# Operand addresses of the matrix products, the order of score groups and one engine choice in a hybrid attention block

## The chip, the cores and the metric

The kernel runs on one core of a Trainium2 chip. The metric is the device time of one execution in microseconds; of the kernel before, three executions were timed (median 804.39, from 802.62 to 804.96). A profile comes from one further execution.

## The reference

One decoder block, 512 tokens, width 2048. A normalised input is projected; half of the heads (A: 8 heads of 128, two key/value heads) use compressed, selected and windowed attention, the other half (B: 16 heads of 64) use a window of 128 with sinks. Each half is gated by a SiLU path, and both go through one output projection.

```python
h = _rmsnorm(x, norm_g[l])
proj = h @ w_in[l]
...
kc = _compress(_rope(_heads(kca, N_KV_A, HEAD_DIM_A)), cmp_k_pos[l], cmp_k_w1[l], cmp_k_w2[l])
vc = _compress(_heads(vca, N_KV_A, HEAD_DIM_A), cmp_v_pos[l], cmp_v_w1[l], cmp_v_w2[l])
o_cmp, p_cmp = _compressed_attention(qa, kc, vc)
sel_idx = _select_blocks(p_cmp, S)
o_sel = _selected_attention(qa, _rope(_heads(ksa, N_KV_A, HEAD_DIM_A)), _heads(vsa, N_KV_A, HEAD_DIM_A), sel_idx)
o_win = _banded_attention(qa, _rope(_heads(kwa, N_KV_A, HEAD_DIM_A)), _heads(vwa, N_KV_A, HEAD_DIM_A), WIN_A)
gates = jax.nn.sigmoid(ga.astype(jnp.float32)).reshape(B, S, N_KV_A, GROUP_A, 3).astype(x.dtype)
o_a = gates[..., 0:1] * o_cmp + gates[..., 1:2] * o_sel + gates[..., 2:3] * o_win
y_a = o_a.reshape(B, S, WIDTH_A) * jax.nn.silu(za)
...
o_b = _banded_attention(qb, _rope(_heads(kb, N_KV_B, HEAD_DIM_B)), _heads(vb, N_KV_B, HEAD_DIM_B),
                        WIN_B, sink=sinks[l].reshape(N_KV_B, GROUP_B))
y_b = o_b.reshape(B, S, WIDTH_B) * jax.nn.silu(zb)
x = x + jnp.concatenate([y_a, y_b], axis=-1) @ w_out[l]
return _rmsnorm(x, final_g)
```

With 512 tokens there are 8 blocks of 64 and 16 may be selected, so every block is, and the selected attention is causal attention over all tokens.

## The kernel before

All of it is one function, `hybrid_block`. A float32 operand is split into two float32r "words", a high word (made on ScalarE, L97 and L542) and the low word that remains (a subtraction on VectorE, L99 and L543). `mm3` (L118 to L121) makes a product of two split operands as three matrix products: high by high, high by low, low by high. Each has a still operand, 128 columns that are loaded into the array, and a moving operand of 256, 280, 288 or 512 columns.

The stages, with their place in the profile:

- 0 to 291 us: projections with the normalised input as the moving operand, 512 columns wide (`proj`, L119 to L121 into `pj`), and the 8 pairs of B heads among them: scores (L349, L350), transposes of the probabilities (L384), values (L389, L390).
- 291 to 316 us, first V stage: `tok_chunk` multiplies tokens (still) by weights (moving, words from `words(MOVING)`), 256 columns wide; among them `compress_unit` (L708, L709) for the compressed keys, words from `words(BELOW)`.
- 316 to 352 us, second V stage: the same with 280 columns (values and gates), among them the compression of the values.
- 352 to 425 us: `seven`, a product of 2x2 blocks in seven block products instead of eight, for the A keys; its words come from `words(STILL)` and stand still, combinations of the input (`xh`, `xl`, `pu`, `qw`) move, 256 columns wide.
- 425 to 665 us: for each A head, `pair` (queries and gate by `seven`; `turn` and `q_split` rotate and split the query, on POOL for heads 0 to 5) and `attn_a`: scores (L932) against the key words `KH`, `KL` in runs of three passes, for each of four query tiles; transposes (L969, L981, L983); values (L975 to L977, L990, L992). A tile scheduler interleaves one head's attention with the next head's `seven`.
- 665 to 801 us: the output projection, y words still, weight words moving, then the final norm.

A run of scores has one, two or three column groups: 288 columns (32 compressed keys and 256 keys), then 256 or 512, then in the last query tile another 256. `step` (L125 to L127) adds one product whose result is not used, with chosen operand addresses, at the start of the first V stage, in `keys` and in the output stage.

Where a tile stands is set by the order in which pools are opened and tiles taken from them; small tiles named `space` move those behind them. `words(place)` cuts 1,024 columns out of tiles of 1,088 at an offset of `place` columns of 4 bytes:

```python
MOVING, EVEN, STILL, BELOW = 0, 16, 32, 48
...
def words(place):
    return [wp.tile([P, 1088], F32R, name=nm, tag=nm)[:, place:place + 1024] for nm in ("whi", "wlo")]
```

Of the kernel before, what the change touches and what calls it, by code (L numbers as in the profile page):

```python
# [10 lines left out]
F32 = mybir.dt.float32  # L11
F32R = mybir.dt.float32r
# [5 lines left out]
P = 128  # L18
S = 512
D = 2048  # L20
KT = D // P
# [6 lines left out]
CMP = 32  # L28
MOVING, EVEN, STILL, BELOW = 0, 16, 32, 48
WARM = 40  # L30
# [5 lines left out]
def hybrid_block(ctx, tc, xT, xtm, w0, wv0, wv1, wz, wq, wo0, wos, cw1, cw2, cpos, e2, rope, tabs, sinks, gT, fg, out):  # L36
# [5 lines left out]

    const = ctx.enter_context(sb("const"))
    wp = ctx.enter_context(sb("wp", bufs=3))
    ident = const.tile([P, P], F32, name="ident")
# [4 lines left out]
    bmask = tab[:, 512 + NQ * CMP:768 + NQ * CMP]  # L50
    small = const.tile([P, 8], F32, name="small")
    rstd, eps = small[:, 0:NQ], small[:, NQ:NQ + 1]
    rstdb = const.tile([P, S], F32, name="rstdb")
    gates = const.tile([P, NQ, 24], F32, name="gates")
    gt = const.tile([P, KT + 1], F32, name="gt")
    rowvalid = gt[:, KT:KT + 1]

# [49 lines left out]
    xpool = ctx.enter_context(sb("xpool", side="right"))  # L107
    xh = xpool.tile([P, KT, S], F32R, name="xh")
    xl = xpool.tile([P, KT, S], F32R, name="xl")
    angles = xstack.enter_context(sb("angles", side="right"))  # L110
# [11 lines left out]

    flat = xh.rearrange("p k s -> p (k s)")

# [19 lines left out]
    def load_x(k):  # L144
        xr = tmp("xr")
        if k == 0:
            nc.sync.dma_start(gt, gT)
        nc.sync.dma_start(xr, xT[:, k, :])
        last["xh"] = act.activation(xh[:, k, :], xr, AF.Copy, scale=gt[:, k:k + 1]).ins
        return xr  # L150
# [48 lines left out]
    with tc.issue_after(last["dma"]):  # L199
        nc.sync.dma_start(cosB, rope[:, 2, :])  # L200
        nc.sync.dma_start(sinB, rope[:, 3, :])
        nc.sync.dma_start(tab, tabs)
    dve.tensor_tensor(out=cosB, in0=cosB, in1=rstdb, op=ALU.mult)
    dve.tensor_tensor(out=sinB, in0=sinB, in1=rstdb, op=ALU.mult)
# [86 lines left out]

    vbf = wb.tile([P, NQ, P], F32, name="vbf")
    sk = wb.tile([P, 5, 16], F32, name="sk")
    nc.sync.dma_start(sk[:, 0, :], sinks)
    act.activation(sk[:, 1, :], sk[:, 0, :], AF.Copy, scale=-1.0)
    KBH = wb.tile([P, 2, S], F32R, name="KBH")
    KBL = wb.tile([P, 2, S], F32R, name="KBL")
    VB = wb.tile([P, NQ, 2, P], F32R, name="VB")
# [34 lines left out]
    def softmax_b(i, q2):  # L333
# [4 lines left out]
        for part in range(2):  # L338
            sums = wk.tile([P, 3, 2, 2], F32, name="sums", tag="sums")
            mn, dn, ex = sums[:, 0], sums[:, 1], sums[:, 2]  # L340
            for e in range(2):
                qt = 2 * part + e
                tt = wb.tile([P, 2, 256], F32, name="ttb", tag="ttb", bufs=6)
                tts.append(tt)
                ko = max(qt - 1, 0) * P
                qs = slice(qt * P, (qt + 1) * P)
                sp = pssb.tile([P, 2, 256], F32, name="spb", tag="spb")
                for v in range(2):
                    pe.matmul(sp[:, v, :], q2[v][:, qs], KBH[:, g, ko:ko + 256], start=v == 0, stop=False)  # L349
                    pe.matmul(sp[:, v, :], q2[v][:, qs], KBL[:, g, ko:ko + 256], start=False, stop=v == 1)  # L350
                n = 256 if qt else 128
                for v in range(2):
                    dve.tensor_tensor_reduce(out=tt[:, v, 0:n], in0=sp[:, v, 0:n], in1=bmask[:, 256 - n:256],
                                             scale=-SCALE_B, scalar=1e38, op0=ALU.add, op1=ALU.min,
                                             accum_out=mn[:, e, v:v + 1])
            dve.tensor_tensor(out=mn, in0=mn, in1=nskb, op=ALU.min)  # L356
            dve.tensor_tensor(out=ex, in0=mn, in1=skb, op=ALU.add)
            act.activation(ex, ex, AF.Exp)
            for e in range(2):
                n = 256 if part or e else 128  # L360
                for v in range(2):
                    tv = tts[2 * part + e][:, v, 0:n]
                    act.activation(tv, tv, AF.Exp, bias=mn[:, e, v:v + 1], scale=-1.0, accum_out=dn[:, e, v:v + 1])  # L363
            dve.tensor_tensor(out=dn, in0=dn, in1=ex, op=ALU.add)
            dve.reciprocal(dn, dn)
            for e in range(2):
                n = 256 if part or e else 128
                for v in range(2):
                    tv = tts[2 * part + e][:, v, 0:n]
                    dve.tensor_scalar(tv, tv, dn[:, e, v:v + 1], None, op0=ALU.mult)  # L370
# [125 lines left out]
    VF = kv.tile([P, 2, 2, 256], F32, name="VF")  # L496
    VC = [kv.tile([P, P], F32R, name=f"VC{g}") for g in range(2)]
    ahead = ExitStack()
    quarters = [ahead.enter_context(sb(f"ahead{e}", side="right")).tile([P, 1024], F32, name=f"ahead{e}") for e in range(2)]
# [171 lines left out]
    def pair(h, hooks=None, extra=None):  # L671
        def q_done(qv):
            turn(qv, engine=pool if h < 6 else dve)
            return q_split(qv, pool if h < 6 else dve)

# [142 lines left out]
    early, ready = quarters[:1], quarters[1:]  # L818
    places = [words(MOVING), words(BELOW), words(BELOW)]

# [24 lines left out]
    for u in range(8):  # L845
# [5 lines left out]
        if u == 0:  # L851
# [3 lines left out]
            cacc[1] = bank(4)  # L855
        compress_unit(1, u, cacc[1], words(BELOW))
        if 1 <= u <= 3:
# [28 lines left out]
    kv = kvstack.enter_context(sb("kvK", side="right"))  # L886
    KH, KL = [kv.tile([P, CMP + 1056], F32R, name=f"K{e}")[:, 0:CMP + 1024] for e in "HL"]
    for e, k in enumerate((KH, KL)):
# [20 lines left out]
    def attn_a(h, qh, ql, st):  # L909
# [4 lines left out]
        for pair in range(2):  # L914
            tt = wa.tile([P, 1792 if pair else 768], F32, name=f"tt{pair}", tag=f"tt{pair}")
            sums = wk.tile([P, 2, 2, 3], F32, name="sums", tag="sums")
            mn, dn = sums[:, 0], sums[:, 1]
            views = []
            off = 0
            for i in range(2):  # L920
# [6 lines left out]
                if qt == 3:  # L927
                    groups.append((1024, 1280, 800))
                qs = slice(qt * P, (qt + 1) * P)
# [70 lines left out]

    yh, yl = [[w[:, (2 * f + 1) % 17, :] for f in range(16)] for w in (xh, xl)]

# [148 lines left out]
    for c, u, ms in ((0, 0, ()), (0, 1, ()), (0, 2, ()), (1, 0, (0, 1, 2)), (1, 1, (3, 4)), (1, 2, (5, 6)), (0, 3, ()),  # L1151
                     (1, 3, (7,))):
        hi, lo = load_unit(wo0[:, c, u], 1024, place=MOVING, loaded=first_units.pop(0) if first_units else None, after=last["qh"],
                           after_lo=low_y[11] if (c, u) == (0, 2) else last["turn"])
# [9 lines left out]
        with tc.issue_after(words_of), tc.issue_after(last["gate", 1]):  # L1164
            for m in ms:
                combos(m)
    banks1 = banks(1)
    step(banks1[3], flat[:, 3 * S - 16:3 * S + 112], flat[:, 2 * S + 32:2 * S + 288])
    for T in range(2):
# [30 lines left out]
    def halves(raw, to=None):  # L1200
        hi, lo = to or words(MOVING)
        split_to(hi, lo, raw)
        return hi, lo
# [5 lines left out]
    for n in range(1, 4):  # L1209
# [117 lines left out]
        else:  # L1327
# [8 lines left out]
            def pair():  # L1336
                return words(MOVING)

# [181 lines left out]
```

## Time and profile before

| | |
|---|---|
| median of three runs | 804.39 us |
| the profiled execution | 802.8 us |
| its span, first to last instruction | 801.0 us |
| mean granted TensorE clock | 0.997 |
| matrix products in it | 5,693 |
| DMA traffic | 131.05 MB, mean 164 GB/s |

The span is what the profile's page and the trace's views divide; 1.8 us of the profiled execution lie around it. A product's recorded duration is longer than the distance to the next one's start, since products are pipelined; the distance is read from two start times, or from a stretch's length and the number of products in it. PE is the matrix product, PEld the load of its still operand, DVE is VectorE, ACT ScalarE, POOL GpSimd, SP the queue engine.

### The profile page before, as it was taken

How to read it: one execution, taken by the hardware profiler on the slowest of the kernel's cores; microseconds unless marked ns; L12 is line 12 of the kernel's file. 1: busy time of each engine (PE TensorE's matmuls, PEld its weight loads, DVE VectorE, ACT ScalarE, POOL GpSimd, SP SyncE). 2: the span in 40 equal slices, each digit the busy share in tenths (PEclk: the TensorE clock that was granted, in tenths of full speed). 3: DMA queues.
4: the chain of work that ended last, by engine and by line, in shares of the span. 5: the costliest groups of instructions: out<-in, count | busy, mean ns of one | idle time of the engine just before them, and what ended most of it. 6: DMA issues, size and time to landing. Idle time of an engine off the chain costs nothing.

```text
span 801.0 us, 15316 instructions
## 1 busy us (share of the span) xinstructions
PE 789.6 (99%) x5693; PEld 739.1 (92%) x5693; DVE 686.3 (86%) x1407; ACT 504.7 (63%) x1103; POOL 108.3 (14%) x111
## 2 busy tenths in 40 slices
PE   9999999999999999999999999999999999999996
PEld 8788888888888899999999999999999999999996
DVE  7668988889989597759999999998999798978895
ACT  6646657655666356664447778777777867553545
POOL 3615002110121000323210110110100000000000
PEclk9999999999999999999999999999999999999998
DMA  7572243564373469887723213225216836797845
GB/s 239 172 242 81 79 144 106 171 171 150 101 210 106 158 200 281 257 269 194 207 82 106 68 53 119 82 92 159 71 50 216 296 120 219 257 266 193 258 86 211
DMA packets 49563, 131.05 MB, mean 164 GB/s; under 512 B 6000, under 2 KB 8848, under 8 KB 49488
## 3 DMA queue, kind: packets, MB, share of 16 engines
q1 hardware_dynamic: 43376, 110.89, 42.3%
q0 software_dynamic: 5824, 18.65, 10.5%
q8 instruction: 45, 0.74, 0.4%
q10 hardware_dynamic: 288, 0.52, 0.2%
q14 instruction: 30, 0.25, 0.1%
HBM read 113.23 MB, written 16.81 MB: 162 GB/s over the span
## 4 chain that ended last, share of the span: by engine, by line
PE 86%; DVE 6%; DMA 3%; ACT 2%; issue 2%; POOL 0%; SPq 0%; DVEq 0%; ACTq 0%
PE pj L119 16%; PE pj L121 15%; PE pj L120 15%; PE oa L120 5%; PE oa L119 5%; PE oa L121 5%; PE sp L932 4%; PE bank L121 2%; PE bank L120 2%; PE bank L119 2%; DMA xr<-xT 2%; DVE wlo L543 2%; PE tp L969 2%; PE tp L384 2%; DMA raw<-wq 1%
## 5 line engine op out<-in xcount | busy, mean ns | idle before, releaser
L119 PE MATMUL pj<-xh,whi 128*128 128x256 f32 (+1 forms) x592 | 196.9, 333 | 0.6 <-ACT t L608 0.5
L121 PE MATMUL pj<-xh,wlo 128*128 128x256 f32 (+1 forms) x592 | 196.2, 331 | 0.0
L120 PE MATMUL pj<-xl,whi 128*128 128x256 f32 (+1 forms) x592 | 196.1, 331 | 0.0
L119 PEld LDWEIGHTS pj<-xh,whi 128*128 128x128 f32 x592 | 111.4, 188 | 11.0 <-ACT t L608 0.9
L121 PEld LDWEIGHTS pj<-xh,wlo 128*128 128x128 f32 x592 | 111.4, 188 | 10.1
L120 PEld LDWEIGHTS pj<-xl,whi 128*128 128x128 f32 x592 | 111.4, 188 | 9.7
L543 DVE TENSOR_TENSOR wlo<-raw,whi 128x1024 fp32r<-128x1024 f32 (+2 forms) x80 | 92.9, 1172 | 7.8 <-ACT whi L542 7.2
L542 ACT ACTIVATE whi<-raw 128x1024 fp32r<-128x1024 f32 (+2 forms) x80 | 77.6, 985 | 30.7 <-DVE raw L581 11.5
L99 DVE TENSOR_TENSOR wlo<-raw,whi 128x1024 fp32r<-128x1024 f32 (+1 forms) x61 | 72.1, 1184 | 22.8 <-ACT whi L97 22.3
L97 ACT ACTIVATE whi<-raw 128x1024 fp32r<-128x1024 f32 (+1 forms) x60 | 56.6, 945 | 28.8 <-PE pj L120 14.8
L120 PE MATMUL oa<-wlo,xh 128*128 128x256 f32 x200 | 55.5, 278 | 0.0
L119 PE MATMUL oa<-whi,xh 128*128 128x256 f32 x200 | 55.4, 278 | 0.0
L121 PE MATMUL oa<-whi,xl 128*128 128x256 f32 x200 | 55.2, 276 | 0.0
L121 PE MATMUL pj<-pu,wlo 128*128 128x256 f32 x160 | 45.0, 281 | 0.5 <-DVE wlo L543 0.5
L119 PE MATMUL pj<-pu,whi 128*128 128x256 f32 x160 | 45.1, 282 | 0.4 <-DVE zr L581 0.4
L120 PE MATMUL pj<-pu,whi 128*128 128x256 f32 x160 | 44.7, 279 | 0.0
L289 DVE TENSOR_TENSOR pl<-tp,ph 128x512 fp32r<-128x512 f32 (+1 forms) x64 | 40.7, 651 | 3.1 <-ACT ph L288 2.9
L288 ACT ACTIVATE ph<-tp 128x512 fp32r<-128x512 f32 (+1 forms) x64 | 34.1, 560 | 9.6 <-PE tp L969 4.4
L363 ACT ACTIVATE ttb<-ttb,sums 128x256 f32<-128x256 f32 (+1 forms) x64 | 30.0, 471 | 14.4 <-DVE sums L356 14.4
L121 PEld LDWEIGHTS oa<-whi,xl 128*128 128x128 f32 x200 | 37.6, 188 | 0.0
L120 PEld LDWEIGHTS oa<-wlo,xh 128*128 128x128 f32 x200 | 37.6, 188 | 0.0
L119 PEld LDWEIGHTS oa<-whi,xh 128*128 128x128 f32 x200 | 37.5, 188 | 0.0
(401 smaller groups left out, 2369.8 us busy)
## 6 DMA issues: line engine op xcount, KB each, us to landing
raw<-wq SPq DMA_DIRECT2D x41, 512.0 KB, 4.4
raw<-wz SPq DMA_DIRECT2D x36, 512.0 KB, 4.0
cw<-cw SPq DMA_DIRECT2D x32, 256.0 KB, 4.0
raw<-wos SPq DMA_DIRECT2D x14, 512.0 KB, 5.9
rw<-wos SPq DMA_DIRECT2D x10, 512.0 KB, 4.8
xr<-xT SPq DMA_DIRECT2D x16, 256.0 KB, 3.4
rows<-xT SPq DMA_DIRECT2D x8, 512.0 KB, 4.7
raw<-wo SPq DMA_DIRECT2D x8, 512.0 KB, 6.0
```

The costliest lines, as they stand in the source:

```text
L97: last["hi"] = act.activation(hi[:, :width], rw[:, :width], AF.Copy).ins
L99: last["lo"] = dve.tensor_tensor(out=lo[:, :width], in0=rw[:, :width], in1=hi[:, :width].bitcast(F32), op=ALU.subtract).ins
L119: pe.matmul(ps, ah, bh, start=first, stop=False, skip_group_check=go_on)
L120: pe.matmul(ps, ah, bl, start=False, stop=False, skip_group_check=go_on)
L121: recent["mm"] = pe.matmul(ps, al, bh, start=False, stop=last, skip_group_check=go_on).ins
L288: act.activation(ph, tp, AF.Copy)
L289: dve.tensor_tensor(out=pl, in0=tp, in1=ph.bitcast(F32), op=ALU.subtract)
L363: act.activation(tv, tv, AF.Exp, bias=mn[:, e, v:v + 1], scale=-1.0, accum_out=dn[:, e, v:v + 1])
L384: pe.transpose(tp[:, o:o + P], tts[kt + s][:, v, c0:c0 + P], ident)
L542: split_hi = act.activation(hi, src, AF.Copy).ins
L543: last["lo"] = dve.tensor_tensor(out=lo, in0=src, in1=hi.bitcast(F32), op=ALU.subtract).ins
L932: pe.matmul(sp[:, a:b], qq[:, qs], kk[:, ko:ko + b - a], start=pi == 0, stop=pi == 2)
```

## The change

The change moves operands to other addresses, changes the order of the column groups in the last query tile's scores, gives head 0's rotation and split to VectorE, and loads one column of the gain tile apart. The number and the shapes of the products are the same.

The addresses modulo 256 bytes, moving operand / still operand, as the built programs have them:

| products | before | after |
|---|---|---|
| 512-wide projections | 192 / 192 | same |
| B scores (L349, L350) | 192 / 0 | same |
| B transposes (L384), B values (L389, L390) | 128 / 192 | 192 / 0 |
| V stages, tokens by weights | 128 / 192 | same |
| compression (L708, L709) | 64 / 128 | 128 / 192 |
| `seven` | 192 / 0 | same |
| A scores, the 288-column group | 192 / 0 | 0 / 0 |
| A scores, the other groups | 64 / 0 | 128 / 0 |
| A transposes, A values | 128 / 192 | 192 / 0 |
| output products | 128 / 192 | 192 / 0 |
| the unused product of the output stage | 64 / 128 | 128 / 192 |

The core of the diff:

```diff
-MOVING, EVEN, STILL, BELOW = 0, 16, 32, 48
+MOVING, EVEN, STILL = 0, 16, 32
...
     const = ctx.enter_context(sb("const"))
+    gt = const.tile([P, KT], F32, name="gt")
...
-    small = const.tile([P, 8], F32, name="small")
+    small = const.tile([P, 16], F32, name="small")
...
-    gt = const.tile([P, KT + 1], F32, name="gt")
-    rowvalid = gt[:, KT:KT + 1]
+    rowvalid = small[:, 8:9]
...
-    xh = xpool.tile([P, KT, S], F32R, name="xh")
-    xl = xpool.tile([P, KT, S], F32R, name="xl")
+    slabs = xpool.tile([P, 2 * KT * S + 64], F32R, name="x")
+    xh, xl = [slabs[:, e * KT * S:(e + 1) * KT * S].rearrange("p (k s) -> p k s", s=S) for e in range(2)]
...
-            nc.sync.dma_start(gt, gT)
+            nc.sync.dma_start(gt, gT[:, 0:KT])
...
         nc.sync.dma_start(tab, tabs)
+        nc.sync.dma_start(rowvalid, gT[:, KT:KT + 1])
...
-    vbf = wb.tile([P, NQ, P], F32, name="vbf")
+    vbf = wb.tile([P, NQ, P], F32, name="vbf", tag="ob")
+    KBH = wb.tile([P, 2, S], F32R, name="KBH")
+    KBL = wb.tile([P, 2, S], F32R, name="KBL")
     sk = wb.tile([P, 5, 16], F32, name="sk")
...
-            sums = wk.tile([P, 3, 2, 2], F32, name="sums", tag="sums")
+            sums = wk.tile([P, 6, 2, 2], F32, name="sums", tag="sums")
...
     VC = [kv.tile([P, P], F32R, name=f"VC{g}") for g in range(2)]
+    kv.tile([P, 48], F32, name="space")
...
         def q_done(qv):
-            turn(qv, engine=pool if h < 6 else dve)
-            return q_split(qv, pool if h < 6 else dve)
+            turn(qv, engine=pool if 0 < h < 6 else dve)
+            return q_split(qv, pool if 0 < h < 6 else dve)
...
-    places = [words(MOVING), words(BELOW), words(BELOW)]
+    places = [words(MOVING) for n in range(3)]
...
-        compress_unit(1, u, cacc[1], words(BELOW))
+        compress_unit(1, u, cacc[1], words(MOVING))
...
-    KH, KL = [kv.tile([P, CMP + 1056], F32R, name=f"K{e}")[:, 0:CMP + 1024] for e in "HL"]
+    KH, KL = [kv.tile([P, CMP + 1056], F32R, name=f"K{e}")[:, 16:CMP + 1040] for e in "HL"]
+    kv.tile([P, 16], F32, name="space")
...
-            sums = wk.tile([P, 2, 2, 3], F32, name="sums", tag="sums")
+            sums = wk.tile([P, 4, 2, 3], F32, name="sums", tag="sums")
...
                 if qt == 3:
-                    groups.append((1024, 1280, 800))
+                    groups.insert(1, (1024, 1280, 800))
...
-    yh, yl = [[w[:, (2 * f + 1) % 17, :] for f in range(16)] for w in (xh, xl)]
+    yh, yl = [[slabs[:, (e * KT + (2 * f + 1) % 17) * S + 16:][:, 0:S] for f in range(16)] for e in range(2)]
...
-        hi, lo = load_unit(wo0[:, c, u], 1024, place=MOVING, ...
+        hi, lo = load_unit(wo0[:, c, u], 1024, place=EVEN, ...
...
+    cmb.tile([P, 48], F32, name="space3")
     banks1 = banks(1)
-    step(banks1[3], flat[:, 3 * S - 16:3 * S + 112], flat[:, 2 * S + 32:2 * S + 288])
+    step(banks1[3], flat[:, 2 * S:2 * S + P], flat[:, 3 * S - 16:3 * S + 240])
...
-        hi, lo = to or words(MOVING)
+        hi, lo = to or words(EVEN)
...
-                return words(MOVING)
+                return words(EVEN)
```

VectorE before, behind the last rotation of head 0 (`t` is the query, `zr` the gate path, `raw` and `wlo` weights of head 1; rows are line, operation, output and inputs, shape):

```order
L581 TENSOR_TENSOR zr<-zr,pj 128x256
L543 TENSOR_TENSOR wlo<-raw,whi 128x1024
L677 TENSOR_TENSOR zr<-zr,rstdb 128x512
L581 TENSOR_TENSOR raw<-raw 128x1024
L682 SCALAR_TENSOR_TENSOR st<-st,zr 128x512
L581 TENSOR_TENSOR raw<-raw 128x1024
```

The same place of VectorE after; a line of before stands here one or two numbers higher:

```order
L583 TENSOR_TENSOR zr<-zr,pj 128x256
L545 TENSOR_TENSOR wlo<-raw,whi 128x1024
L666 TENSOR_TENSOR t_4495<-t_4495,t_4691 128x512
L679 TENSOR_TENSOR zr<-zr,rstdb 128x512
L583 TENSOR_TENSOR raw<-raw 128x1024
L262 TENSOR_TENSOR ql<-t_4495,qh 128x512
L684 SCALAR_TENSOR_TENSOR st<-st,zr 128x512
L583 TENSOR_TENSOR raw<-raw 128x1024
```

The rotation's last addition stands ahead of the gate path's product, the query's low word behind it and one addition of weights; both were POOL's. On TensorE, the scores of head 0's last query tile before, with the product of head 1's projection on each side:

```order
L121 MATMUL pj<-xh,wlo 128x256
L932 MATMUL sp<-KH,qh 128x288
L932 MATMUL sp<-KH,qh 128x512
L932 MATMUL sp<-KH,qh 128x256
L932 MATMUL sp<-KL,qh 128x288
L932 MATMUL sp<-KL,qh 128x512
L932 MATMUL sp<-KL,qh 128x256
L932 MATMUL sp<-KH,ql 128x288
L932 MATMUL sp<-KH,ql 128x512
L932 MATMUL sp<-KH,ql 128x256
L119 MATMUL pj<-xh,whi 128x256
```

and the same run after:

```order
L121 MATMUL pj<-x,wlo 128x256
L935 MATMUL sp<-KH,qh 128x288
L935 MATMUL sp<-KH,qh 128x256
L935 MATMUL sp<-KH,qh 128x512
L935 MATMUL sp<-KL,qh 128x288
L935 MATMUL sp<-KL,qh 128x256
L935 MATMUL sp<-KL,qh 128x512
L935 MATMUL sp<-KH,ql 128x288
L935 MATMUL sp<-KH,ql 128x256
L935 MATMUL sp<-KH,ql 128x512
L119 MATMUL pj<-qw_608,whi 128x256
```

Each pass now ends with 512 columns, and the run stands one `mm3` of head 1's projection later. From here on the scheduler's interleaving of attention and projection differs in places; behind the last attention the output stage's products stand in the same order.

More of the change, by code (lines that the diff above doesn't have):

```diff
@@ L121, in mm3 @@
         recent["mm"] = pe.matmul(ps, al, bh, start=False, stop=last, skip_group_check=go_on).ins
-    flat = xh.rearrange("p k s -> p (k s)")
+    flat = slabs[:, 0:KT * S]
     def step(bank, still, moving):
@@ L295, in hybrid_block @@
     act.activation(sk[:, 1, :], sk[:, 0, :], AF.Copy, scale=-1.0)
-    KBH = wb.tile([P, 2, S], F32R, name="KBH")
-    KBL = wb.tile([P, 2, S], F32R, name="KBL")
     VB = wb.tile([P, NQ, 2, P], F32R, name="VB")
@@ L1152, in hybrid_block @@
                      (1, 3, (7,))):
-        hi, lo = load_unit(wo0[:, c, u], 1024, place=MOVING, loaded=first_units.pop(0) if first_units else None, after=last["qh"],
+        hi, lo = load_unit(wo0[:, c, u], 1024, place=EVEN, loaded=first_units.pop(0) if first_units else None, after=last["qh"],
                            after_lo=low_y[11] if (c, u) == (0, 2) else last["turn"])
```

## The prediction

> **What bounds the kernel now.** I read the page first: the span, the busy shares, the granted clock and the chain of work that ended last.
>
> ```profile
> span 801.0 us, 15316 instructions
> PE 789.6 (99%) x5693; PEld 739.1 (92%) x5693; DVE 686.3 (86%) x1407; ACT 504.7 (63%) x1103; POOL 108.3 (14%) x111
> PEclk9999999999999999999999999999999999999998
> PE 86%; DVE 6%; DMA 3%; ACT 2%; issue 2%; POOL 0%; SPq 0%; DVEq 0%; ACTq 0%
> ```
>
> TensorE never stops for long and its clock is granted in full, so the time is the number of matrix products times the distance from one start to the next. The change neither adds nor removes a product. What it can save is in that distance, and this is not the same everywhere, as the windows view shows (length, PE busy and, in brackets, how many products fall in it):
>
> ```profile
> 297.00:316.00 19.00, 19.00 (x164) 1.00 0.93 279
> 700.00:790.00 90.00, 90.00 (x795) 1.00 0.73 201
> ```
>
> 90.00/795 is 113.2 ns for each, 19.00/164 is 115.9, and both stretches hold only products 256 columns wide, without a pause. The view of one line (count, then duration minimum/median/maximum) and the groups by form (count, busy, mean duration) tell the two kinds apart:
>
> ```profile
> L121 PE MATMUL oa<-whi,xl x161: 276/276/278, 665.0 to 779.3; 128*128 128x256 f32 x161
> ...
> L120 PE MATMUL pj<-xl,whi x207: 276/279/368, 425.9 to 618.8; 128*128 128x256 f32 x104
> L120 PE MATMUL pj<-pu,whi x104: 276/279/369, 429.4 to 608.0; 128*128 128x256 f32 x104
> L120 PE MATMUL oa<-wlo,xh x37: 276/281/365, 646.9 to 662.6; 128*128 128x256 f32 x37
> ...
> L976 PE MATMUL op<-pl,VH x64: 276/281/366, 444.3 to 663.1; 128*128 128x256 f32 x64
> ```
> ```profile
> L120 PE MATMUL bank<-wlo,xh 128*128 128x256 f32 x41 | 11.5, 282 | 0.0
> L121 PE MATMUL bank<-whi,xl 128*128 128x256 f32 x41 | 11.5, 281 | 0.0
> L119 PE MATMUL bank<-whi,xh 128*128 128x256 f32 x41 | 11.3, 281 | 0.0
> ```
>
> A product of this width is recorded at 276 ns or at 281 ns, and with 281 the next one starts some 118 ns later and not 113. I call the first tight and the second loose. In the output stage (665 to 779) all are tight; in the first V stage (297 to 316, last fence) practically all are loose; in the attention stage (425 to 663) the medians lie between, about half are loose. The longest, near 369, are products behind a transpose; their time is the transpose's.
>
> What decides the pace is seen in the timeline, around the one product of L975 that attention puts among the projection's (start, duration):
>
> ```profile
> 453.54 0.28 PE L119 MATMUL pj<-xh,whi 128*128 128x256 f32 x1
> 453.65 0.28 PE L975 MATMUL op<-ph,VH 128*128 128x256 f32 x1
> 453.77 0.28 PE L120 MATMUL pj<-xl,whi 128*128 128x256 f32 x1
> 453.89 0.28 PE L121 MATMUL pj<-xh,wlo 128*128 128x256 f32 x1
> 454.01 0.28 PE L119 MATMUL pj<-xh,whi 128*128 128x256 f32 x1
> 454.13 0.28 PE L120 MATMUL pj<-xl,whi 128*128 128x256 f32 x1
> 454.24 0.28 PE L121 MATMUL pj<-xh,wlo 128*128 128x256 f32 x1
> ```
>
> Fast before (0.11), four distances of 0.12 from L975 on, then tight again. Nothing is waited for there. What differs is the place of the operands, and the next rows say why two places meet:
>
> ```profile
> 299.83 0.28 PE L120 MATMUL bank<-wlo,xh 128*128 128x256 f32 x1
> 299.83 0.19 PEld L121 LDWEIGHTS bank<-whi,xl 128*128 128x128 f32 x1
> ```
>
> The next product's still operand is read from the moment the running one starts to read its moving operand. I call the start address of the first less that of the second, modulo 256 bytes, the step. By the addresses of the built program the rows at 453.54 have steps 0 (L119 to L975), then 128 (L975 to L120), all others 64. So a chain of 64s keeps its pace; 0 turns tight into loose; 128 after it turns it back. A loose chain of 64s stays loose for dozens of products. Behind a run of key products the same shows:
>
> ```profile
> 435.36 0.64 PE L932 MATMUL sp<-KH,ql 128*128 128x288 f32 x3
> ...
> 436.07 0.28 PE L121 MATMUL pj<-xh,wlo 128*128 128x256 f32 x1
> 436.19 0.28 PE L119 MATMUL pj<-qw,whi 128*128 128x256 f32 x1
> 436.31 0.28 PE L120 MATMUL pj<-qw,whi 128*128 128x256 f32 x1
> ```
> ```profile
> 632.27 0.53 PE L932 MATMUL sp<-KH,ql 128*128 128x288 f32 x2
> ...
> 633.00 0.28 PE L121 MATMUL pj<-whi,xl 128*128 128x256 f32 x1
> 633.11 0.28 PE L119 MATMUL pj<-whi,xh 128*128 128x256 f32 x1
> 633.22 0.28 PE L120 MATMUL pj<-wlo,xh 128*128 128x256 f32 x1
> ```
>
> The first run ends with a step of 192 and leaves the loose pace (0.12 on), the second ends with 128 and is followed by the tight one.
>
> **The change part by part.** I sum against the profiled execution, 802.8 us (span 801.0 and 1.8 around it); the median of the three runs is 804.39, so it stands 1.6 below, and the sum is carried over to the median.
>
> First V stage, 297 to 316. The compression products' words sat 64 bytes apart from those of the V products, so each change between them was a step of 0 or 128; now all are 64, behind an opening step of 0 and 128 that is there already. By the three rows 41 x (6 + 5 + 5) = 656 ns are lost; nothing hides them, since TensorE is the chain. I take 0.6 (a stall or two will bring a few loose ones back); the ends are 0 and 0.7.
>
> Second V stage, 316 to 352. Products of 280 columns are no whole number of 64 bytes, and keep their pace as it is. The compression products between them stand at
>
> ```profile
> L708 PE MATMUL bank<-whi,F 128*128 128x256 f32 x28 | 7.1, 280 | 0.0
> ```
>
> so with as many of its partner line some 56 x 4 = 0.2 us; I take 0.1, as the 280s before them disturb whatever the steps; ends 0 and 0.3.
>
> Attention, 425 to 665. Counted one by one in the timeline, 738 of 1,574 products of 256 columns (key products left out) are loose, at 4.7 ns each 3.5 us; the medians above agree with half. What turns them: steps of 0 and 128 around every block of attention (all gone: transposes, softmax, V and words now stand at 64 to each other), key runs, and transposes and pauses, which remain. The key runs now have a step of 0 at each product of 288 columns and 128 at each other one, and three-group runs end with 512 columns. So 24 of 32 end with 128, as at 632.27. I choose that the loose ones fall to about 300, nearer to none than to all, since two of the three kinds of trigger go or turn: 438 x 4.7 = 2.0 us. The ends are 0 (transposes alone bring the loose pace) and 3.5. No row shows 288 columns with a step of 0. The nearest are 453.65 (256 columns, step 0, 5 ns lost) and the key products' own neighbours at 436.07, which lose 5 ns now: with 96 of them that is 0.5 us more if each comes to lose it, 0.5 less if each ceases to, and I take 0, since both rows are equally near.
>
> Window attention, before 291: its 80 value products change their place, the 512-wide projections around them keep their step of 0. At the same 5 ns the ends are 0 and 0.4; I take 0, since the changes between steps of 0 and 64 remain. Output, 665 to 801: tight before, its step stays 64, so 0 if it starts tight (the rival below is where not).
>
> Head 0 on VectorE. Two instructions leave POOL and go to VectorE:
>
> ```profile
> 414.63 1.23 DVE L543 TENSOR_TENSOR wlo<-raw,whi 128x1024 fp32r<-128x1024 f32 x1
> 415.77 0.69 DVE L662 TENSOR_TENSOR t<-t,cosA 128x512 f32<-128x512 f32 x1
> 416.61 1.28 POOL L664 TENSOR_TENSOR t<-t,t 128x512 f32<-128x512 f32 x1 [21.54 <-DVE t L662]
> 416.70 2.27 DVE L543 TENSOR_TENSOR wlo<-raw,whi 128x1024 fp32r<-128x1024 f32 x1
> 418.64 1.49 POOL L261 TENSOR_TENSOR ql<-t,qh 128x512 fp32r<-128x512 f32 x1 [0.75 <-ACT qh L260]
> 418.90 1.78 DVE L677 TENSOR_TENSOR zr<-zr,rstdb 128x512 f32<-128x512 f32 x1
> 420.85 0.29 PE L932 MATMUL sp<-KH,ql 128*128 128x288 f32 x1
> 421.66 0.39 PE L119 MATMUL pj<-xh,whi 128*128 128x256 f32 x1 [0.52 <-ACT t L608]
> ```
>
> Beside POOL, L543 took 2.27 where it takes 1.23 alone, and L677 1.78 where L662 of the same shape takes 0.69: VectorE loses 2.1 us to POOL and now gets two more of 0.7, so it is 0.7 us ahead. The product at 421.66 started 0.81 us after the key product before it, where 0.13 would do: its bank waited for ACT's copy L608, queued behind the tanh that waits for L677. L677 comes earlier, so most of 0.7 goes. Next in line is the low word of the query: it now stands behind L677 and a 1.2 us addition on VectorE, from the end of L543 at 416.7 + 1.2 that is 417.9 + 0.7 + 0.7 + 1.2 + 0.7 = 421.2, where the keys want it at 420.85. So 0.3 of waiting replaces 0.7: I take 0.4; ends 0.8 less and, if the low word slips behind one more 1.2 us addition, 0.5 more.
>
> The gain tile's load loses its last column, which gets a load of its own behind the tables: one more issue on SP, of 128 numbers. What reads them is the gates' evacuation, after both V stages, so other work covers it: 0; uncovered it would be one small transfer.
>
> Sum: 0.6 + 0.1 + 2.0 + 0.4 = 3.1 us; 802.8 becomes 799.7, and the median 804.39 becomes 801.3.
>
> **The rivals.** (a) Addresses are not the cause, the loose pace only goes along with them. The Trainium skill, "TensorE: Matmul & The Clock Gate", section "Step-by-step: what each phase is for", says that the array has two independent read ports and that loading the next still operand takes nothing from the running product; by that rule the sum would be the 0.4 of head 0. The trace speaks against it: 276 and 281 in one shape, with no wait, as at 453.65. For (a) speaks that loose chains also begin behind pauses. Then only head 0's 0.4 is left: 804.39 - 0.4 = 804.0.
>
> (b) The V stages gain, attention doesn't, because transposes and pauses bring the loose pace back as often as before: 0.6 + 0.1 + 0.4 = 1.1, so 803.3. For it: at 436.07 no block of attention stands near.
>
> (c) Slower: a chain keeps the pace it gets. From the last head's transposes on, 1,106 output products now follow with steps of 64 alone, and one pair of 0 and 128. If they enter loose and the pair does not turn them, they cost 1,106 x 4.7 = 5.2 us, where they cost nothing now; with (b)'s 1.1, and attention gaining nothing, 804.39 + 4.1 = 808.5. To be slower by over 0.3% (2.4 us) beside (b)'s 1.1, some 745 of them must stay loose (3.5 us at 4.7 ns). Against it: the same pair sits there now and leaves the tight pace.
>
> (d) The scheduler's new order in attention (it moves whole runs of products) opens a new wait of 1 us or so: it lies within the range.
>
> **How the numbers follow.** Forecast 0.52, (a) 0.15, (b) 0.22, (c) 0.11. Likeliest 801.3. All gains at their ends, 0.7 + 0.3 + 3.5 + 0.5 + 0.4 + 0.8 = 6.2, give 798.2, and some 1 us less for a run like the lowest of before, 1.8 under its median; upward (a) with head 0 and the keys at their bad ends is 804.39 + 1.0 = 805.4. The range 797.3 to 805.4 leaves (c) out. 0.3% (2.4 us) is about what a measurement of this kernel can tell from no change: the forecast (3.1, mostly beyond it) gives faster 0.54 with a little of (b); (a), most of (b) and the forecast's weak edge 0.35; slower 0.11.
>
> **What would show it.** Right: in the V stage the three lines' medians at 276; in attention medians of 276 for L120 and L976's successors; L677's successor at 0.7 us and no pause at 421; the output stage unchanged at 276. Wrong: medians of 281 behind key runs or in the output stage, or a pause over 0.8 us at the first keys.

## The result, and the profile after

| kernel | median us | lowest to highest | to the kernel before |
|---|---|---|---|
| before | 804.38 | 802.62 to 804.96 | |
| changed | 815.25 | 811.31 to 816.77 | 1.0131 [1.0092, 1.0171] |

The change costs 10.9 us; forecast were 801.3 and a range up to 805.4. The profiled execution of the changed kernel took 816.77 us, its highest, so it stands 14.0 above the profiled one of before.

The page of the changed kernel, with the lines that answer to those of before:

```profile
span 815.0 us, 15335 instructions
PE 797.2 (98%) x5693; PEld 742.9 (91%) x5693; DVE 682.8 (84%) x1409; ACT 504.6 (62%) x1103; POOL 106.7 (13%) x109
PEclk9999999999999999999999999999999999999998
PE 72%; DVE 13%; ACT 5%; DMA 5%; issue 4%; POOL 0%; SPq 0%; ACTq 0%; DVEq 0%; POOLq 0%
```

The clock is as before and VectorE has no more work than before (682.8 against 686.3), yet its share of the chain that ends last has gone from 6% to 13%: TensorE now waits for it. The waits of TensorE from 420 to 800 us (waiter, what it waits for, us in total, times, longest) say where, first in the kernel before, then in the changed one:

```profile
PE pj L119 <- ACT t L608: 0.5, 1, 0.5
PE sp L932 <- DVE sums L938: 0.2, 1, 0.2
```
```profile
PE pj L121 <- DVE wlo L545: 1.7, 3, 0.8
PE pj L119 <- ACT whi L544: 1.1, 2, 0.9
PE pj L119 <- ACT x L1050: 1.1, 1, 1.1
PE oa L120 <- DVE wlo L1055: 0.7, 1, 0.7
PE sp L935 <- DVE sums L941: 0.6, 2, 0.4
PE sp L935 <- POOL ql L262: 0.4, 1, 0.4
PE op L979 <- DVE pl L290: 0.2, 1, 0.2
```

0.7 us of waiting have become 5.8. (The changed file is 2 to 4 lines longer: L121 of before is still L121, L932 is L935, L1052 is L1055.) The view counts only time in which nothing ran at all. Counted by start times, as the distance to the next start less that of a tight product of the same width, the whole difference is seen. A distance of over 30 ns too much is a pause here, a smaller one is a loose product; transposes are counted apart and differ by less than 0.5 us in all.

| us | before: pauses, loose | changed: pauses, loose |
|---|---|---|
| 20 to 290 | 1.6, 2.3 | 4.2, 2.5 |
| 290 to 352 (V stages) | 0.1, 1.9 | 0.3, 1.0 |
| 352 to 420 | 2.4, 0.7 | 1.9, 0.9 |
| 420 to 672 (attention) | 1.3, 4.3 | 6.3, 4.2 |
| from 672 (output) | 0.2, 0.0 | 2.6, 4.7 |

Of the 14.0 us, 9.6 are pauses and 4.1 loose products. The 2.6 at the start go with the execution, not with the change: the kernels below have pauses of 0.9 to 4.6 us there, the highest of them in a kernel with the old start (e10). What every kernel with the new order shows again (e1, e3, e4 and e12 below) is some 4.5 to 5.5 us more of pauses in attention and 2 to 3 in the output stage, and in most of them its loose products. Such counts are of one trace each, and a trace is one execution. These stand in the window of 700 to 790 us (length, PE busy, in brackets the products), here of the changed kernel:

```profile
700.00:790.00 90.00, 90.00 (x766) 90.00 (x766) 73.84 (x83) 42.12 (x53) 8.55 (x10) 1.00 0.74 198
```

766 products where the kernel before has 795 in the same time, 90.00/766 = 117.5 ns each instead of 113.2. Where the chain of products lost its pace is seen in the timeline of the changed kernel (start, duration; in brackets the idle time and what ended it):

```profile
693.20 0.28 PE L120 MATMUL oa<-wlo,ph 128*128 128x256 f32 x1
693.32 0.28 PE L121 MATMUL oa<-whi,pl 128*128 128x256 f32 x1
694.29 0.39 PE L120 MATMUL oa<-wlo,x 128*128 128x256 f32 x1 [0.69 <-DVE wlo L1055]
694.51 0.28 PE L121 MATMUL oa<-whi,x 128*128 128x256 f32 x1
694.63 0.28 PE L119 MATMUL oa<-whi,x 128*128 128x256 f32 x1
```

Tight (0.11) up to a pause of 0.97 us, loose (0.12) from it on, to the last product. The pair of steps that stands at 688 us had just made the chain tight.

The pauses of the output stage have a visible cause. VectorE's last instruction of attention, in the kernel before and in the changed one:

```profile
664.23 0.69 DVE L270 SCALAR_TENSOR_TENSOR yp<-op,st 128x512 f32<-128x512 f32 x1 [0.38 <-PE op L992]
```
```profile
674.67 0.69 DVE L271 SCALAR_TENSOR_TENSOR yp<-op,st 128x512 f32<-128x512 f32 x1 [2.97 <-PE op L995]
```

Attention ends 10.4 us later, since the last head's last value product stands 30 places later among the products (3.4 us) and TensorE is by then some 7 us behind. What VectorE and ScalarE still have to make of the last head's result, and then the output's weight words, stands in line behind it.

### The profile page after: what moved, and what is told of

It is laid out like the page before. It is cut to its first block, busy times and chain, and to the rows that moved or that the text cites. A ratio compares the mean times of both kernels' runs of the same rounds, so it can differ in the third digit from the quotient of the medians.

```text
span 815.0 us, 15335 instructions
## 1 busy us (share of the span) xinstructions
PE 797.2 (98%) x5693; PEld 742.9 (91%) x5693; DVE 682.8 (84%) x1409; ACT 504.6 (62%) x1103; POOL 106.7 (13%) x109
## 3 DMA queue, kind: packets, MB, share of 16 engines
q0 software_dynamic: 5824, 18.65, 10.5%
## 4 chain that ended last, share of the span: by engine, by line
PE 72%; DVE 13%; ACT 5%; DMA 5%; issue 4%; POOL 0%; SPq 0%; ACTq 0%; DVEq 0%; POOLq 0%
PE pj L121 13%; PE pj L119 13%; PE pj L120 13%; PE oa L120 4%; PE oa L121 4%; PE oa L119 4%; DVE wlo L545 3%; PE bank L121 2%; PE bank L120 2%; PE bank L119 2%; PE sp L935 2%; DMA raw<-wq 2%; DVE raw L583 2%; PE tp L385 2%; DMA xr<-xT 1%
## 5 line engine op out<-in xcount | busy, mean ns | idle before, releaser
L119 PE MATMUL pj<-x,whi 128*128 128x256 f32 (+1 forms) x592 | 197.1, 333 | 1.2 <-ACT whi L544 0.9
L121 PE MATMUL pj<-x,wlo 128*128 128x256 f32 (+1 forms) x592 | 196.1, 331 | 0.8 <-DVE wlo L545 0.8
L120 PE MATMUL pj<-x,whi 128*128 128x256 f32 (+1 forms) x592 | 196.2, 331 | 0.0
L119 PEld LDWEIGHTS pj<-x,whi 128*128 128x128 f32 x592 | 111.4, 188 | 11.7 <-ACT whi L544 1.1
L121 PEld LDWEIGHTS pj<-x,wlo 128*128 128x128 f32 x592 | 111.4, 188 | 11.0 <-DVE wlo L545 1.0
L120 PEld LDWEIGHTS pj<-x,whi 128*128 128x128 f32 x592 | 111.5, 188 | 9.9
L545 DVE TENSOR_TENSOR wlo<-raw,whi 128x1024 fp32r<-128x1024 f32 (+2 forms) x80 | 91.1, 1150 | 11.1 <-ACT whi L544 10.6
L120 PE MATMUL oa<-wlo,x 128*128 128x256 f32 x200 | 56.4, 282 | 0.7 <-DVE wlo L1055 0.7
L121 PE MATMUL oa<-whi,x 128*128 128x256 f32 x200 | 56.2, 281 | 0.0
L119 PE MATMUL oa<-whi,x 128*128 128x256 f32 x200 | 56.2, 282 | 0.0
L121 PE MATMUL pj<-pu,wlo 128*128 128x256 f32 x160 | 45.0, 281 | 1.2 <-DVE wlo L545 1.2
L120 PE MATMUL pj<-pu,whi 128*128 128x256 f32 x160 | 44.5, 278 | 0.0
L120 PEld LDWEIGHTS oa<-wlo,x 128*128 128x128 f32 x200 | 37.6, 188 | 0.9 <-DVE wlo L1055 0.9
L119 PEld LDWEIGHTS oa<-whi,x 128*128 128x128 f32 x200 | 38.1, 191 | 0.0
L121 PEld LDWEIGHTS oa<-whi,x 128*128 128x128 f32 x200 | 37.7, 188 | 0.0
```

The source lines that it names most:

```text
L119: pe.matmul(ps, ah, bh, start=first, stop=False, skip_group_check=go_on)
L120: pe.matmul(ps, ah, bl, start=False, stop=False, skip_group_check=go_on)
L121: recent["mm"] = pe.matmul(ps, al, bh, start=False, stop=last, skip_group_check=go_on).ins
L545: last["lo"] = dve.tensor_tensor(out=lo, in0=src, in1=hi.bitcast(F32), op=ALU.subtract).ins
```

## The experiments

Each ratio is to the kernel before as measured beside the run on the same chip (medians 803.0 to 803.7), so runs are best compared by it.

| run | edit | median us | ratio to the kernel before |
|---|---|---|---|
| e1 | before + head 0 on VectorE | 814.40 | 1.0126 [1.0104, 1.0148] |
| e2 | changed, without head 0 and group order | 803.75 | 0.9998 [0.9987, 1.0009] |
| e3 | before + head 0 + group order | 814.02 | 1.0134 [1.0110, 1.0158] |
| e4 | changed + second pair of steps | 812.15 | 1.0107 [1.0090, 1.0124] |
| e5 | e2 + probability words 64 bytes lower | 804.27 | 1.0009 [0.9997, 1.0020] |
| e6 | before + head 1 on VectorE | 811.70 | 1.0100 [1.0083, 1.0117] |
| e7 | before + head 0's split on VectorE | 809.98 | 1.0078 [1.0063, 1.0094] |
| e8 | before + 16 copies on VectorE | 811.65 | 1.0106 [1.0081, 1.0131] |
| e9 | before + head 5 on VectorE | 805.35 | 1.0024 [1.0011, 1.0036] |
| e10 | before + V stage's addresses | 803.45 | 0.9998 [0.9985, 1.0011] |
| e11 | before + head 0 on VectorE, old order | 802.94 | 1.0001 [0.9989, 1.0013] |
| e12 | before, in the order of e1 | 813.58 | 1.0121 [1.0098, 1.0145] |
| e13 | changed, in the order of before | 805.29 | 1.0024 [1.0006, 1.0042] |
| e14 | e13 + second pair of steps | 804.12 | 1.0009 [0.9993, 1.0026] |

### The two halves of the change: e1, e2, e3

The scheduler's order hangs on which engine an instruction runs on, not on addresses: with head 0 and the groups put back, every engine's list is that of before. So the change falls into an order and a set of addresses.

e1 and, with the second line too, e3:

```diff
-            turn(qv, engine=pool if h < 6 else dve)
-            return q_split(qv, pool if h < 6 else dve)
+            turn(qv, engine=pool if 0 < h < 6 else dve)
+            return q_split(qv, pool if 0 < h < 6 else dve)
...
-                    groups.append((1024, 1280, 800))
+                    groups.insert(1, (1024, 1280, 800))
```

e2 is the changed kernel without these two edits.

> The kernel before with one edit: head 0's rotation and split on VectorE. Every address is that of before; the scheduler's order is that of the changed kernel but for the key runs of three groups. Theory S (the new order opens the waits, about 9.6 us of them in the trace of after): 9 to 14 us over the kernel before, with pauses at the same places, 447, 457, 600, 679 and 693 us. Theory A (the new addresses make the time, the waits are a by-product): within 2 us of the kernel before, at best the 0.4 us gain of the prediction.

> The changed kernel with head 0 back on GpSimd and the old order of the score groups, so that every engine has the instruction order of before and only addresses and the gain column's load differ. Theory S: no new pauses, 0.5 to 3 us under the kernel before (first V stage tight, output stage tight). Theory A: 4 us or more over it, with the output products loose (281 ns).

> The kernel before with head 0 on VectorE and the new order of the score groups: the order of instructions of the changed kernel on every engine, the addresses of before. Theory S: 9 to 14 us over the kernel before; if pauses alone turn a chain loose, the output products are loose here too behind the pause at 693 us (about 4 us of the sum). Theory A: within 2 us of the kernel before.

The order carries the loss, 10.9 and 10.5 us, and the addresses bring nothing that can be measured, either way: TensorE's list in e2 is that of before, product for product. The pauses of e1 and e3 stand where those of the changed kernel stand (447, 457, 517, 601, 679 and 693 us, within 3 us). In e3 the pause at 693 left the chain tight, in e1 loose, with the same addresses and a pause of the same length (0.89 us): what decides the pace behind a pause is not shown.

### The loose output stage: e4

```diff
             product(bb, [halves(r) for r in r22], "22", True)
...
+            if n == 1:
+                step(banks1[3], flat[:, 2 * S:2 * S + P], flat[:, 3 * S - 16:3 * S + 240])
             product(ba, [halves(c) for c in ch], "12", False)
```

> The changed kernel with one unused product more: a second pair of steps of 0 and 128 in the output stage, some 97 products behind the first, about 6 us behind the pause at 693 us. If a pause turned the chain loose and the pair turns it tight again: some 830 products from 276 instead of 281 ns, 830 x 4.7 = 3.9 us under the changed kernel, about 811. If the loose pace there has another cause: no change, about 815.

812.15, 3.1 us under the changed kernel; each taken against the kernel before that was measured beside it, the difference is 2.2 (8.7 and 10.9 us over), and the two intervals overlap, so the time alone does not settle it. The traces do: from 672 us on, loose products cost 4.7 us in the changed kernel and 0.7 in e4. (All four executions of e4 lie between 811.6 and 813.1; of the changed kernel's, one lies at 811.3 and three from 814.7 up, as they would if the pause left the chain tight in one of them; only one of each was profiled, so this is not shown.) The timeline of e4 around the product that was added (L127):

```profile
698.72 0.28 PE L121 MATMUL oa<-whi,x 128*128 128x256 f32 x1
698.84 0.28 PE L127 MATMUL oa<-x 128*128 128x256 f32 x1
698.96 0.28 PE L120 MATMUL oa<-wlo,x 128*128 128x256 f32 x1
...
699.66 0.28 PE L120 MATMUL oa<-wlo,x 128*128 128x256 f32 x1
699.77 0.28 PE L121 MATMUL oa<-whi,x 128*128 128x256 f32 x1
699.89 0.28 PE L119 MATMUL oa<-whi,x 128*128 128x256 f32 x1
700.00 0.28 PE L120 MATMUL oa<-wlo,x 128*128 128x256 f32 x1
```

0.12 before it and for five more products, then 0.11 to the end: the pair does turn a loose chain, with a delay of some products. Behind them, with steps of 64 alone, the chain keeps the tight pace, as the changed kernel's keeps the loose one.

### Attention's loose products: e5

```diff
-        ph, pl = [wk.tile([P, S], F32R, name=nm, tag=nm)[:, 0:tp.shape[-1]] for nm in ("ph", "pl")]
+        ph, pl = [wk.tile([P, S + 64], F32R, name=nm, tag=nm)[:, 48:48 + tp.shape[-1]] for nm in ("ph", "pl")]
```

> The kernel of e2 (order of before, new addresses) with the probability words, the moving operand of the value products, 64 bytes lower, and nothing else: the step into a value product stays 64, the step out of it becomes 128; no step of 0 comes back into attention. Theory R (a step of 128 resets a loose chain some 4 to 7 products later, and the change took these resets away together with the steps of 0): the loss to loose products in 425 to 675 us falls from 4.2 us in e2 to 2 to 3 us, so 1 to 2 us under e2, about 802. Theory N (transposes and pauses alone decide, steps do little): unchanged, 803.75 within 0.9.

Theory R's number did not come: 804.27, and the loose products of 420 to 672 us cost 5.1 us in its trace, 4.1 in e2's. But the edit does more than was meant: where one value product follows another, the step is now 128 too. Of these products 115 of 139 are loose in e5, 58 of 141 in e2. At the end of such a block, where a projection product follows, theory R's reset is seen: 19 of 27 chains were loose just behind the step, and 15 of the 19 turned tight 4 to 7 products later. In all, the steps of 128 cost more here than they brought; a version with that step at the end of a block alone was not run.

### Order or load: e6 to e9

e6 and e9 move head 1 or head 5 instead of head 0, e7 moves half of head 0's work. e8 gives VectorE that much work more without moving anything:

```diff
         def q_done(qv):
+            if h == 0:
+                for n in range(16):
+                    dve.tensor_copy(spare0, qv[:, 0:32])
```

> The kernel before with the rotation and split of head 1, not head 0, on VectorE: the same two instructions more for VectorE, another order (the last value product stands 10 products later than before; with head 0 it is 30). Theory L (the load on VectorE makes the waits): 9 to 14 us over the kernel before, as in e1. Theory O (the order that the scheduler lays out makes them, and how late it ends attention decides the two pauses of the output stage): another set of pauses, less than e1, 0 to 7 us over.

> The kernel before with only the split of head 0 (one instruction of 0.7 us) on VectorE, the rotation stays on GpSimd; the last value product stands 8 products earlier than before. Theory L: about half of e1, 5 to 7 us over the kernel before. Theory O: no pause near 1 us at 679 and 693 us, at most a few in attention: 0 to 3 us over.

> The kernel before with 16 copies of 128x32 numbers more on VectorE, behind head 0's query (about 1.2 us of VectorE time, as much as the change adds), whose results nobody reads; TensorE's order stays that of before but for 14 rows around head 0. Theory L (VectorE's load makes the waits): 5 us or more over the kernel before, pauses in later heads too. Theory O (the new order makes them): at most the copies' own 1.2 us at head 0, where the query waits behind them, and no new pause behind 435 us.

> The kernel before with rotation and split of head 5, not head 0, on VectorE. TensorE's order is that of before up to 572 us and differs behind it. Theory O: pauses as in before up to 572 us (1 us in all from 425), new ones of some 1 to 4 us behind it. Theory L: as much as in e1 for the same two instructions, 9 us or more.

Their totals decide nothing: e7 (6.3 us over) and e8 (8.6) lie in theory L's ranges, e9 (2.3) in theory O's, e6 (8) in neither. The pauses say more. e6 has other ones than e1 (2.3 us at 510). In e7 attention ends early enough, and the two pauses of the output stage are gone as theory O has it, but those of attention are all there (6.3 us), with half the load. e9 fits O: no new pause up to 572 us, where its order begins to differ, one of 0.99 at 597.

e8 was built badly. Eight of the copies went ahead of the query's own multiplication:

```profile
420.96 1.69 DVE L675 COPY space<-t 128x32 f32<-128x32 f32 x8
422.68 0.69 DVE L662 TENSOR_TENSOR t<-t,cosA 128x512 f32<-128x512 f32 x1
```
```profile
425.50 0.61 PE L935 MATMUL sp<-KH,qh 128*128 128x288 f32 x1 [4.98 <-ACT qh L260]
```

In the kernel before L662 starts at 415.77. So the keys waited for the query, 5.0 us and more at one place, where 1.2 were expected. Its total says nothing of either theory; that no new pause follows behind 435 us speaks for O.

### Order and engine taken apart: e11 and e12

What was wanted is head 0 on VectorE in the old order, and the new order with head 0 on GpSimd. A table of the old list (PINNED, per engine the instructions' numbers) and an edge between neighbours of one engine make the scheduler keep a given order:

```diff
+    for engine, gaps in json.loads(zlib.decompress(base64.b85decode(PINNED))).items():
...
+            if ahead_of is not None:
+                tc.add_manual_dep(i, ahead_of.name, mybir.DependencyInfo(mybir.DependencyClass.NoSync, mybir.DependencyReason.DATA),
+                                  reason="pinned")
+            ahead_of = i
```

> The kernel before with head 0's rotation and split on VectorE, and a table that keeps every engine's instructions in the order of before (edges between neighbours of one engine, no waits): only the two instructions have left GpSimd's list and stand in VectorE's. Theory O (the new order makes the waits, not where head 0's two instructions run): 0 to 0.5 us under the kernel before, the pause at 421 us from 0.7 to some 0.35 us, no other new pause. Theory L (VectorE's load makes them): 9 us or more over it, as in e1.

> The counterpart: the kernel before with head 0 on GpSimd as before, and a table that keeps every engine's instructions in the order of e1. Theory O: 8 to 13 us over the kernel before, pauses at 447, 457, 517, 601, 679 and 693 us as in e1. Theory L: within 2 us of the kernel before.

This settles it. TensorE's list is that of before in e11 and that of e1 in e12, product for product. Its waits from 420 to 800 us in e11, then in e12 (the table makes both files some 70 lines longer):

```profile
PE sp L1004 <- DVE sums L1010: 0.2, 1, 0.2
```
```profile
PE pj L192 <- DVE wlo L614: 1.5, 3, 0.8
PE pj L190 <- ACT xh L1118: 1.1, 1, 1.1
PE pj L190 <- ACT whi L613: 0.8, 1, 0.8
PE oa L191 <- DVE wlo L1123: 0.7, 1, 0.7
PE sp L1003 <- DVE sums L1009: 0.7, 2, 0.5
...
PE sp L1003 <- POOL ql L332: 0.3, 1, 0.3
```

With head 0 on VectorE in the old order nothing new waits, 802.94 us. With every instruction on its old engine and at its old address, the new order alone gives 813.58, the changed kernel's waits (5.8 us over the whole view), and a loose output stage (4.5 us of loose products from 672 us on).

What such an order does is seen at head 1's first keys. The kernel before, GpSimd's subtraction (the query's low word) first:

```profile
443.29 2.31 POOL L261 TENSOR_TENSOR ql<-t,qh 128x512 fp32r<-128x512 f32 x1 [0.75 <-ACT qh L260]
...
445.40 0.38 PE L932 MATMUL sp<-KH,qh 128*128 128x288 f32 x1
445.62 0.29 PE L932 MATMUL sp<-KL,qh 128*128 128x288 f32 x1
445.75 0.28 PE L121 MATMUL pj<-pu,wlo 128*128 128x256 f32 x1
...
446.89 0.29 PE L932 MATMUL sp<-KH,ql 128*128 128x288 f32 x1
```

The changed kernel, again the subtraction first:

```profile
445.54 2.08 POOL L262 TENSOR_TENSOR ql<-t,qh 128x512 fp32r<-128x512 f32 x1 [0.74 <-ACT qh L261]
...
446.89 0.29 PE L935 MATMUL sp<-KH,qh 128*128 128x288 f32 x1
447.02 0.29 PE L935 MATMUL sp<-KL,qh 128*128 128x288 f32 x1
447.67 0.40 PE L935 MATMUL sp<-KH,ql 128*128 128x288 f32 x1 [0.36 <-POOL ql L262]
448.30 0.38 PE L979 MATMUL op<-pl,VH 128*128 128x256 f32 x1 [0.23 <-DVE pl L290]
```

Before, ten projection products stand between the keys' second pass and the third, which needs the query's low word, and the third starts 1.3 us after the subtraction has ended. In the new order none stand there, so TensorE stands still until the subtraction ends, though it takes no longer than before (2.08 and 2.31 us), and again for the value product behind it, which waits for VectorE's split: 1.0 us at one place, as in e12 at 444.5.

### The V stage alone: e10

```diff
-        F = wk.tile([P, 4, P], F32R, name="F", tag=("ph", "pl")[u % 2])
+        F = wk.tile([P, S + 64], F32R, name="F", tag=("ph", "pl")[u % 2])[:, 16:16 + S].rearrange("p (j c) -> p j c", c=P)
...
-    places = [words(MOVING), words(BELOW), words(BELOW)]
+    places = [words(MOVING) for n in range(3)]
...
-        compress_unit(1, u, cacc[1], words(BELOW))
+        compress_unit(1, u, cacc[1], words(MOVING))
```

To make room, vbf shares the tag "ob", as in the change.

> The kernel before with the address part of the V stage alone: compression words where the V words are, their still operand 64 bytes higher, so that all steps of 291 to 352 us are 64; nothing else moves, every engine keeps its order. By the prediction's first two terms 0.6 to 0.7 us under the kernel before (loose products in 290 to 352 us fall from 1.85 to 1.05 us in the trace), with 276 ns as the median of the three lines into bank; if the V stage's gain is given back behind it: same.

803.45, the same, and in its trace the loose products of 290 to 352 us still cost 1.8 us. The reason stands in its timeline:

```profile
300.86 0.28 PE L709 MATMUL pj<-wlo,F 128*128 128x256 f32 x1
...
301.20 0.38 PE L120 MATMUL bank<-wlo,xh 128*128 128x256 f32 x1
301.42 0.28 PE L121 MATMUL bank<-whi,xl 128*128 128x256 f32 x1
301.54 0.28 PE L119 MATMUL bank<-whi,xh 128*128 128x256 f32 x1
```

It enters tight and passes the compression products tight, as meant; one pause of 0.11 us (301.20 to 301.42, where 0.11 would do) leaves it loose, and with steps of 64 alone it stays so to the end of the first V stage.

### Do the parts add up: e13 and e14

e13 is the changed kernel with the table of the old order (the score groups' swap kept); e14 adds e4's pair.

> The whole changed kernel (its addresses, its score groups, head 0 on VectorE, the gain column's own load), with a table that keeps every engine's instructions in the order of before but for the score groups' own swap. If the order is all of the loss and nothing is lost where it meets the addresses: the two halves add up, e2 (same) and e11 (same), 801.5 to 804.5 us. If the new addresses cost something with head 0 on VectorE that neither half shows: 806 or more.

> e13 with the second pair of steps of e4, 97 products behind the first. If the 2 us that e13 stands over the kernel before are executions in which a pause behind the first pair leaves the output stage loose (up to 5 us in each): the highest executions go, spread within 802 to 806, median about 803.5. If they come from elsewhere (the start, the B heads, attention): 805.3 and the same spread as e13, 802 to 810.

e13 takes back some 9 of the 10.9 us, but at 805.29 it stands between the two expectations, 2 us over the kernel before, interval 0.5 to 3.4, with a spread of 802.4 to 809.9. e14 lies 1.2 lower with a spread of 801.8 to 807.7; the two intervals overlap, so whether a loose output stage in some executions makes these 2 us stays open. No version was found that beats the kernel before.

## Why the prediction was wrong, point by point

**The step that failed** is rival (d): "The scheduler's new order in attention (it moves whole runs of products) opens a new wait of 1 us or so: it lies within the range." The new order was known, its effect was put at one wait and given no chance of its own. It opened about ten, 5 us in attention and 2.4 in the output stage, and through the last of them a loose output stage: 10.45 us by e12 against the kernel before on the same chip (813.58 and 803.13), where nothing but the order differs. A sign that the prediction had named for being wrong came with it: 281 ns as the median of the output products (L120 and L121 into `oa` in the changed kernel). The prediction read the time of each wait from the old trace, and the old trace shows only what the old order covers.

**Head 0 on VectorE, 0.4 us.** About right at its place: the product behind the keys starts 0.48 us after the key product in the changed kernel (422.63 to 423.11) and in e11, 0.81 before, so half of the pause is left; the low word's wait, put at 0.3, is 0.1. In the sum of e11 it is too small to be measured.

**First V stage, 0.6 us.** Right in kind and size where the chain comes through tight. The three lines of the changed kernel in the groups by form (count, busy, mean ns):

```profile
L120 PE MATMUL bank<-wlo,x 128*128 128x256 f32 x64 | 17.7, 278 | 0.0
L121 PE MATMUL bank<-whi,x 128*128 128x256 f32 x64 | 17.6, 276 | 0.0
L119 PE MATMUL bank<-whi,x 128*128 128x256 f32 x64 | 17.5, 276 | 0.0
...
L710 PE MATMUL bank<-whi,F 128*128 128x256 f32 x32 | 8.1, 280 | 0.0
```

276 to 278, where the same lines have 280 and 281 over all 64 before; and loose products of 290 to 352 us fall from 1.9 to 1.0 or 1.1 us in the changed kernel, e2, e4, e5, e13 and e14. e10 shows that it is not certain. The second term's 0.1 did not come: L708's 280 is still 280 (L710, last row).

**Attention, 2.0 us.** The term was mis-sized; by the means below it is 0.3 to 0.4, within their scatter. With the old addresses loose products cost 4.3 to 5.2 us from 420 to 672 us (before, e1, e3, e6 to e12), mean 4.7, with the new ones 4.1 to 4.7 (the changed kernel, e2, e4, e13), mean 4.4. I had chosen 300 loose products "since two of the three kinds of trigger go or turn". The third was enough: behind transposes, counted in the traces of the changed kernel, e2 and e4, 32 of 43 tight chains came out loose, and 37 of 56 loose ones stayed so. That steps of 0 do harm is right: of 26 tight chains that met one in the trace of before, from 290 us on, all 26 were loose behind it (or behind the 128 that followed at once). But the rule that 0 loosens and 128 repairs was half of it: all six loose chains of that trace that met a 0 with only 64s behind it (at 303, 311, 318, 480, 572 and 603 us) were tight some four products later. So a step of 0 turned the chain whichever pace it had. And most of the steps of 0 were followed by a 128, at once or at the end of the block, and 18 of the 27 chains that were loose behind a 128 turned tight 4 to 7 products later. The pairs that the change took away were trigger and repair in one.

**Rival (a)** named the Trainium skill's rule that the array's two read ports are independent ("TensorE: Matmul & The Clock Gate", section "Step-by-step: what each phase is for"). Taken at its word, no place of one operand against the other could change the pace; the V stage's 281 and 276 without a wait, and the rows around e4's L127, 0.12 apart and then 0.11, speak against it. What makes the two paces is not shown. The rival's price for the addresses, nothing, was right by luck: in e2's trace the V stage gains 0.8 us, and loose products of 352 to 420 us and from 672 us on take 0.6 of it back.

**Rival (c)** had the right mechanism and the wrong place. I asked whether the chain would enter the output stage loose and whether the pair would turn it. It entered loose and the pair did turn it; a pause behind the pair undid it. 4.7 us of loose products were seen, 5.2 priced.

**The range** left out what is beyond it: it summed bounds of the terms that had been thought of, and the order's own bound, all pauses that a cover of a few products had prevented, was not among them.

## What to carry to other kernels

Where a scheduler lays out the work from modelled times, moving one instruction to another engine can replace the order of everything behind it (in e9 from 570 us on): price the new order as a change of its own, or keep the old order by edges within each engine and measure the two apart. In a kernel that is bound by TensorE, an instruction that feeds it is safe only as long as other products stand between its end and its use; look at these distances in the new order for every head, not at the place of the edit alone. An address pattern that merely keeps a good pace gains only where no pause breaks it; a product that restores the pace belongs behind the last pause, not ahead of it.

## What the runs showed of the hardware that was not expected

- The pace that a chain of 256-column products keeps can be lost to a pause as short as 0.11 us (e10), and need not be lost to one of 0.89 (e3). Behind the pause near 693 us the changed kernel, e1, e4 and e12 were loose, e3 tight.
- A step of 128 works with a delay: the products behind it are mostly loose at first and tight 4 to 7 later (before: 18 of 27; e5 at the end of a block: 15 of 19; e4, a 0 and a 128 together: five later).
